# A hybrid decoder layer on one core: branch tiles read through a ring of five buffers, merge weights fetched earlier

## The chip, the cores and the metric

The kernel runs on one core of one Trainium2 chip. Its time is the device time of one execution in microseconds. Three runs of the kernel before took 1553.57, 1547.87 and 1562.55 us; the median, 1553.57 us, is the time to which everything is compared.

The names of the engines: PE is the matmul engine (PEld its weight load), ACT and DVE the two engines that copy, split and reduce, POOL a third such engine that also issues gathers, SP an engine that only issues transfers. ACT issues transfers too; "ACTq" and "SPq" in a row are an engine's issue of a transfer.

## The reference, cut to what matters

One inference step of one layer for a prompt of 512 tokens and, with the same weights, for 8 samples of one new token each that have 4096 past tokens in a paged cache. All is fp32.

```python
h = rmsnorm(x, g_norm1) * (1.0 + sc1) + sh1
u = einsum('btd,df->btf', h, w_in)
u_rx, u_ry, u_qkv, u_z, u_a, u_b, u_mq, u_mkv, u_gate = split(u, offs, axis=-1)
o_rg  = rglru_branch(u_rx, u_ry, ...)      # causal conv of width 4, gates, linear recurrence
o_gdn = gdn_branch(u_qkv, u_z, ...)        # causal conv of width 4, gated delta rule
cq   = rmsnorm(u_mq);  q = cq @ w_uq       # MLA_HEADS = 8, Q_LORA = 384
c_kv = rmsnorm(u_mkv[..., :256])           # keys c_kv @ w_uk, values c_kv @ w_uv
o_mla = attend(q_nope, q_rope, c_kv, k_rope, w_ukv)
m = (sigmoid(ga) * (o_rg @ w_rg_proj)      # 1280 -> 1024
     + sigmoid(gb) * (o_gdn @ w_gdn_proj)  # 1024 -> 1024
     + sigmoid(gc) * (o_mla @ w_mla_proj))
x = x + gt1 * (m @ w_o)                    # then the SwiGLU block
```

`attend` is causal attention over the 512 prompt tokens for the prompt, and for each sample attention over its 32 cache pages of 128 tokens and its own new token, in the latent space of 256 + 32 numbers.

## The kernel before, in words

Activations stand with features on the 128 partitions and the 520 tokens (512 of the prompt, 8 samples) along the free dimension, in two halves of 260. An fp32 product is made of three: each operand is split into a high and a low fp32r part, by a copy on ACT and a subtraction on DVE. `split` (L154) does so for a weight tile (`raw` to `whi` at L158 and `wlo` at L159), `hilo` (L175) for an activation tile (`brh` at L179, `brl` at L180). `load` (L149) fetches a weight tile into one of two buffers tagged `raw`; `wload` is load and split.

The program's parts in time, read from the trace:

- 0 to about 480 us: norm, the input projection and the gated delta branch. Every conv input tile takes its state of 35 columns by a copy at L383 (on POOL), 512 columns by ACT (L384) and 8 by DVE (L386).
- 480 to 735 us: the recurrent branch and the gate columns of the input projection. From here to about 985 us the sample attention runs in between, one step at a time: `steps(n)` adds n to what is due and runs as many steps of it. A step is, for instance, `scores` (L1107): 24 matmuls of a page block `cc` into the PSUM tile `sp`, a maximum (L1114, DVE) and a copy to SBUF (`SC`, L1115, ACT); or `sa`, the sum over pages `cv`. Pages come by SP (L1085) and, three of eight, as gathers by POOL (L1080); `cv` are gathers of POOL.
- 735 to 806 us: the MLA projections of the prompt. `bf` tiles of the latents (`d_ck`, `d_cq`) are read by SP through two buffers and split (ck0h, cq0h, ...); then `values` (L1293) with `w_uv`, then for four head pairs the keys with `w_uk` (L1335) and the queries with `w_uq` (L1342), each weight by a `wload` on ACT's queue.
- 806 to 914 us: prompt attention, a loop over 16 pairs of (head pair, query block) that runs two ahead with scores (`h` at L1359), one ahead with transposes (L1377), and then `ho` (L1387). In rounds 8 to 12 `branch` (L1277) reads a tile of the recurrent branch's output (`d_ro`) into one of two buffers `bf` and splits it.
- 914 to about 1040 us: the merges. `merge` multiplies the branch tiles by `w_rg` (ten k-tiles, two weight tiles of 640 columns for each of eight output tiles), then `w_gdn`, then `w_mla`, scaled by the gates (`tg`). `fetch` reads and splits the branch tiles just before each merge. After that come `w_o` and the SwiGLU block, to the end.

A tile scheduler fixes each engine's order of instructions at build time, and each engine runs its queue in that order. In the MLA and merge parts the weight and branch loads stand on ACT's queue, between ACT's copies; the page loads stand on SP's. Each load of SP or ACT signals one of eight semaphores, taken in turn, and where the load before on that semaphore might still be under way, the issuing engine first waits for it.

## Time and profile before

| what | value |
|---|---|
| median of 3 runs | 1553.57 us (1547.87 to 1562.55) |
| the profiled execution's own time | 1555.39 us |
| its span, first to last instruction | 1553.6 us |
| mean granted clock of PE | 0.975 of full speed |
| PE busy | 1479.3 us, 95% of the span |
| DVE, ACT, POOL busy | 818.9, 643.1, 243.2 us |
| mean transfer rate | 165 GB/s over the span |

The profiled execution is 1.82 us above the median of the three runs. A busy time is that of one engine; what an engine that is not the last to be ready spends idle costs nothing. The releaser in brackets is what ended the idle time in front of an instruction. The clock column gives the granted clock as a share of full speed.

### The profile page before, as it was taken

The page shows a single profiled execution, that of the slowest core. Times are in us where ns is not written, and L with a number is a line of the kernel's source. Part 1 is how long each engine was busy: PE and PEld are TensorE (multiplying, and loading weights), DVE is VectorE, ACT ScalarE, POOL GpSimd, SP SyncE. Part 2 cuts the span into 40 slices and gives each one's busy share as a digit, 9 for nine tenths or more (in the row PEclk, how much of TensorE's full clock was granted, in tenths as well). Part 3 has the DMA queues.
Part 4 walks back from the last instruction along what each step waited for, and adds up shares of the span by engine and source line. Part 5 has one row for each costly group of instructions (what it writes and reads, how often), then busy time and mean ns, then how long its engine had stood idle before and what let it go on. Part 6 is the DMA issues. An engine that isn't in the chain of part 4 may idle for free.

```text
span 1553.6 us, 33507 instructions
## 1 busy us (share of the span) xinstructions
PE 1479.3 (95%) x13348; PEld 1346.7 (87%) x13348; DVE 818.9 (53%) x1938; ACT 643.1 (41%) x1226; POOL 243.2 (16%) x391
## 2 busy tenths in 40 slices
PE   8999999999998999999878889999999999999997
PEld 5799999999987988887665559999999999999997
DVE  4577865857755676765344424464464333333333
ACT  4464644644533777564334433232243222222233
POOL 0121000100103444333323532000000000000001
PEclk7999999999998999999889999999999999999998
DMA  8234142351436966877777978676743223323222
GB/s 344 83 112 122 58 127 95 97 155 61 125 117 196 270 194 210 275 235 249 241 234 198 265 248 292 192 240 216 270 151 109 84 86 86 103 93 95 84 84 93
DMA packets 117774, 255.98 MB, mean 165 GB/s; under 512 B 22281, under 2 KB 53770, under 8 KB 117618
## 3 DMA queue, kind: packets, MB, share of 16 engines
q1 hardware_dynamic: 83904, 161.85, 33.0%
q0 software_dynamic: 13824, 47.72, 9.9%
q10 hardware_dynamic: 19890, 44.27, 8.8%
q8 instruction: 105, 1.72, 0.5%
q14 instruction: 51, 0.42, 0.1%
HBM read 228.61 MB, written 25.18 MB: 163 GB/s over the span
## 4 chain that ended last, share of the span: by engine, by line
PE 51%; DMA 4%; issue 2%; ACT 2%; DVE 1%; another core or an unknown queue 1%; SPq 0%; POOL 0%; ACTq 0%; POOLq 0%; DVEq 0%
PE mm L172 40%; PE sp L1112 2%; PE sa L1144 1%; DMA bf<-d_ro 1%; PE s L224 1%; PE ho L1387 1%; PE h L1359 1%; DMA St<-in_S 1%; PE mm L1312 1%; DMA bf<-d_cq 1%; PE h L1377 1%; DMA out_gS_s<-St 1%; PE s L888 1%; DMA raw<-in_w_rg 1%
## 5 line engine op out<-in xcount | busy, mean ns | idle before, releaser
L158 ACT ACTIVATE whi<-raw 128x1024 fp32r<-128x1024 f32 (+3 forms) x204 | 199.5, 979 | 506.9 <-PE mm L172 443.6
L159 DVE TENSOR_TENSOR wlo<-raw,whi 128x1024 fp32r<-128x1024 f32 (+3 forms) x204 | 229.1, 1124 | 232.4 <-ACT whi L158 226.4
L172 PE MATMUL mm<-hh,whi 128*128 128x260 f32 x1312 | 281.1, 292 | 4.9 <-ACT hh L295 2.7
L172 PE MATMUL mm<-hh,wlo 128*128 128x260 f32 x1312 | 273.5, 287 | 0.1
L172 PE MATMUL mm<-hl,whi 128*128 128x260 f32 x1312 | 272.9, 287 | 0.7 <-DVE hl L295 0.6
L172 PEld LDWEIGHTS mm<-hh,whi 128*128 128x128 f32 x1312 | 206.8, 191 | 16.6 <-issue 7.9
L172 PEld LDWEIGHTS mm<-hl,whi 128*128 128x128 f32 x1312 | 206.1, 191 | 3.2 <-issue 2.1
L172 PEld LDWEIGHTS mm<-hh,wlo 128*128 128x128 f32 x1312 | 206.1, 191 | 3.0 <-issue 1.4
L172 PE MATMUL mm<-h2h,whi 128*128 128x260 f32 x704 | 144.5, 284 | 0.0
L172 PE MATMUL mm<-h2h,wlo 128*128 128x260 f32 x704 | 144.1, 283 | 0.0
L172 PE MATMUL mm<-h2l,whi 128*128 128x260 f32 x704 | 143.6, 283 | 0.0
L1080 POOL DMA_INDIRECT cc<-in_ckvT,pkx x96 | 101.6, 1058 | 129.6 <-PE sp L1112 74.3
L172 PE MATMUL mm<-brh,whi 128*128 128x260 f32 x556 | 114.2, 287 | 5.1 <-ACT brh L179 4.9
L172 PE MATMUL mm<-brl,whi 128*128 128x260 f32 x556 | 113.0, 284 | 0.7 <-issue 0.6
L172 PE MATMUL mm<-brh,wlo 128*128 128x260 f32 x556 | 112.3, 284 | 0.0
L172 PEld LDWEIGHTS mm<-h2h,whi 128*128 128x128 f32 x704 | 109.3, 188 | 2.9 <-issue 2.5
L172 PEld LDWEIGHTS mm<-h2h,wlo 128*128 128x128 f32 x704 | 109.4, 188 | 0.4 <-issue 0.4
L172 PEld LDWEIGHTS mm<-h2l,whi 128*128 128x128 f32 x704 | 109.1, 188 | 0.4 <-DVE h2l L1549 0.4
L172 PEld LDWEIGHTS mm<-brh,whi 128*128 128x128 f32 x556 | 86.0, 189 | 11.0 <-ACT brh L179 6.0
L172 PEld LDWEIGHTS mm<-brl,whi 128*128 128x128 f32 x556 | 85.9, 189 | 1.6 <-DVE mx L1120 0.8
L172 PEld LDWEIGHTS mm<-brh,wlo 128*128 128x128 f32 x556 | 86.0, 189 | 0.3 <-issue 0.2
L1610 POOL TENSOR_TENSOR x<-x,rf 128x260 f32<-128x260 f32 x6 | 4.3, 736 | 514.7 <-ACT rf L1607 514.7
(522 smaller groups left out, 2500.7 us busy)
## 6 DMA issues: line engine op xcount, KB each, us to landing
raw<-in_w_in SPq DMA_DIRECT2D x55, 512.0 KB
wa<-in_w_ada SPq DMA_DIRECT2D x48, 512.0 KB
cc<-in_ckvT SPq DMA_DIRECT2D x160, 144.0 KB
raw<-in_w_f SPq DMA_DIRECT2D x44, 512.0 KB
raw<-in_w_in ACTq DMA_DIRECT2D x27, 512.0 KB
raw<-in_w_f SPq DMA_DIRECT2D x16, 384.0 KB
d_g<-gt ACTq DMA_DIRECT2D x22, 260.0 KB
raw<-in_w_rg ACTq DMA_DIRECT2D x16, 320.0 KB
```

What stands on the lines that cost most here:

```text
L158: A.activation(hi[:, :n], raw[:, :n], AF.Copy)
L159: V.tensor_tensor(lo[:, :n], raw[:, :n], hi[:, :n], ALU.subtract)
L172: TE.matmul(pt[:, a, 0:HB], w[:, k * 128:k * 128 + 128], x[k0 + k][:, a * HB:(a + 1) * HB], start=start and k == 0 and i == 0, stop=stop a ...
L224: TE.matmul(pt[32 * j:32 * j + 32, 0:256], sc[:, k, :], wa[:, j * 256:(j + 1) * 256], start=k == 0, stop=k == 7)
L888: TE.matmul(pw[:, 0:272], a_[:, sl], b_[:, ca], start=i == 0, stop=i == 2)
L1080: G.indirect_dma_start(ct[:, i].rearrange("p c t -> p (c t)"), None, I["ckvT"], bass.IndirectOffsetOnAxis(ap=pkx[0:96, o:o + 1], axis=0))
L1112: TE.matmul(po[32 * j:32 * j + 32, 0:256], Qst[:, t, 4 * self.g + j, :], cts[j][:, :, t, :], start=t == 0, stop=t == 2)
L1144: TE.matmul(self.pa[32 * j:32 * j + 32, 0:256], self.PTt[:, t * 128 + 32 * j:t * 128 + 32 * j + 32], self.vts[j][:, t * 256:(t + 1) * 256] ...
L1312: TE.matmul(pt[:, a, 0:256], a_[:, c0 + k * 128:c0 + k * 128 + 128], x[:, a * HB:a * HB + 256], start=k == 0 and i == 0, stop=k == n - 1 a ...
L1359: TE.matmul(pS[:, 0:n], qts[2 * p + u][:, b * 128:n], kts[p][:, u, 0:n], start=True, stop=False)
L1377: TE.transpose(pT[:, kb * 128:(kb + 1) * 128], Ps[u][:, kb * 128:(kb + 1) * 128], ident)
L1387: TE.matmul(po[u][:, b * 128:(b + 1) * 128], vv[:, kb, hd * 128:(hd + 1) * 128], PTs[u][:, kb * 128:(kb + 1) * 128], start=kb == 0, stop=k ...
```

## The change

What it does, in the order of the diff:

1. The copy of the conv state (L383) goes from POOL to DVE.
2. In a sample score step, ACT's copy of the PSUM tile comes first, and DVE takes the maximum from that copy in SBUF.
3. `branch` is cut in two: `branch_load` reads a tile into a ring, `branch` splits the oldest. During attention and the first merge the ring has five buffers in a pool of its own; ten `d_ro` and eight `d_og` loads are listed in `ahead`, and `send(1)` issues the next: in rounds 3 to 7 without a split, afterwards one for each split. The `d_og` tiles are split between the output tiles of the first merge, no longer in a block behind it. The 8 sample columns are copied by DVE, no longer by POOL.
4. The MLA weights have buffers of their own (four `ruk`, two `ruq`), filled ahead; the `w_uv` loads are named earlier; the latents' `bf` has three buffers. So the two `raw` buffers come free for the first two `w_rg` tiles.
5. In attention `steps(STEPS[1])` (0.7 of a step) also runs in the two rounds that fill the pipeline, so 1.4 steps more in all lie ahead of the loop's end.
6. `fetch` is used for the `d_om` tiles alone, with two buffers.

```diff
--- before.py
+++ after.py
@@ -380,7 +380,7 @@
 
             cin = p.tile([128, 548], F32, tag="cin", name="cin", bufs=2)
             y2 = p.tile([128, CW], F32, tag="cw", name="cz", bufs=6)
-            G.tensor_copy(cin[:, 0:35], state)
+            V.tensor_copy(cin[:, 0:35], state)
             A.activation(view2(cin[:, 35:547]), pt[:, :, 0:256], AF.Copy)
             seg = cin[:, 0:32].rearrange("p (a b c) -> p a b c", a=2, b=4)
             V.tensor_copy(seg[:, :, :, 3], pt[:, :, 256:260])
@@ -1111,8 +1111,8 @@
                     for j in range(4):
                         TE.matmul(po[32 * j:32 * j + 32, 0:256], Qst[:, t, 4 * self.g + j, :], cts[j][:, :, t, :],
                                   start=t == 0, stop=t == 2)
-                V.reduce_max(self.mx[:, blk:blk + 1], po[:, 0:256], axis=AX.X)
                 A.activation(self.SC[:, blk * 256:(blk + 1) * 256], po[:, 0:256], AF.Copy)
+                V.reduce_max(self.mx[:, blk:blk + 1], self.SC[:, blk * 256:(blk + 1) * 256], axis=AX.X)
 
             def weights(self):
                 st, mx, part = self.st, self.mx, self.part
@@ -1274,14 +1274,21 @@
     px = es.enter_context(pool("px"))
     xs = {}
 
-    def branch(p, n, src, k, samples):
-
-        f = p.tile([128, NT], F32, tag="bf", name="bf", bufs=2)
+    raw_ring = []
+
+    def branch_load(p, src, k, samples, bufs):
+
+        f = p.tile([128, NT], F32, tag="bf", name="bf", bufs=bufs)
         if samples is None:
             queue[0].dma_start(f, src[k])
         else:
             queue[0].dma_start(pr(f), src[k].rearrange("p (a b) -> p a b", a=2))
-            G.tensor_copy(sm(f), samples[:, k, :].rearrange("p (a b) -> p a b", a=2))
+            V.tensor_copy(sm(f), samples[:, k, :].rearrange("p (a b) -> p a b", a=2))
+        raw_ring.append(f)
+
+    def branch(p, n):
+
+        f = raw_ring.pop(0)
         xs[n] = hilo(px, f, "br", bufs=5) if n % 18 < 5 else hilo(p, f, "br", bufs=13)
 
     with ExitStack() as sub:
@@ -1291,7 +1298,7 @@
         kts, qts = [], []
 
         def values(lat):
-            uvs = [wload(I["w_uv"][c], 1024) for c in range(2)]
+            uvs = [split(r, 1024) for r in raws]
             for b in range(4):
                 pt = mm_tile()
                 for c in range(2):
@@ -1319,9 +1326,24 @@
             csq = pl.tile([128, 2, 512], F32, name="csq")
             krp = pl.tile([128, 512], F32, name="krp")
             lat = {}
+
+            raws = [load(I["w_uv"][c], 1024) for c in range(2)]
+            ruk, ruq = [], []
+
+            def key_load(p):
+                ruk.append(pl.tile([128, 256], F32, tag="ruk", name="ruk", bufs=4))
+                queue[0].dma_start(ruk[-1], I["w_uk"][p])
+
+            def query_load(p):
+                ruq.append(pl.tile([128, 768], F32, tag="ruq", name="ruq", bufs=2))
+                queue[0].dma_start(ruq[-1], I["w_uq"][p])
+
+            for p in range(2):
+                key_load(p)
+                query_load(p)
             for nm, src, n in (("ck", d_ck, 2), ("cq", d_cq, 3)):
                 for i in range(n):
-                    f = pl.tile([128, NT], F32, tag="bf", name="bf", bufs=2)
+                    f = pl.tile([128, NT], F32, tag="bf", name="bf", bufs=3)
                     SP.dma_start(f, src[i])
                     lat[nm, i] = hilo(pl, f, f"{nm}{i}", bufs=1)
             SP.dma_start(csq, I["csq"])
@@ -1332,14 +1354,17 @@
             V.tensor_copy(mbf[:, 1], pt[:, 0:128])
             values(lat)
             for p in range(4):
-                pt = lat_gemm(lat, wload(I["w_uk"][p], 256), 0, "ck", 2)
+                pt = lat_gemm(lat, split(ruk[p], 256), 0, "ck", 2)
                 kt = ph.tile([128, 2, 512], F32, name=f"kt{p}")
                 for u in range(2):
                     lo_, hi_ = slice(64 * u, 64 * u + 64), slice(64 - 64 * u, 128 - 64 * u)
                     A.activation(view2(kt[lo_, u]), pt[lo_, :, 0:256], AF.Copy)
                     V.tensor_copy(kt[hi_, u], krp[hi_])
                 kts.append(kt)
-                wq = wload(I["w_uq"][p], 768)
+                wq = split(ruq[p], 768)
+                if p < 2:
+                    key_load(p + 2)
+                    query_load(p + 2)
                 for u in range(2):
                     pt = lat_gemm(lat, wq, u * 384, "cq", 3)
                     qt = ph.tile([128, 512], F32, name=f"qt{p}{u}")
@@ -1348,6 +1373,15 @@
                 steps(STEPS[5])
 
         pp = sub.enter_context(pool("pp"))
+
+        pr_ = smp.enter_context(pool("pr", side="right"))
+        ahead = [(d_ro, k, None) for k in range(10)] + [(d_og, k, osf) for k in range(8)]
+
+        def send(n):
+            for a in ahead[:n]:
+                branch_load(pr_, *a, 5)
+            del ahead[:n]
+
         psum(sub, "psh", h=4, ho=2)
         spare[0] = lambda: s_tile("h")
 
@@ -1400,11 +1434,14 @@
                 PTs[i + 1] = turn(order[i + 1][1], Ps.pop(i + 1))
             if i + 2 < 16:
                 Ps[i + 2] = scores(*order[i + 2])
+            steps(STEPS[1])
             if i < 0:
                 continue
-            steps(STEPS[1])
+            if 3 <= i < 8:
+                send(1)
             if 8 <= i < 13:
-                branch(pp, i - 8, d_ro, i - 8, None)
+                branch(pp, i - 8)
+                send(1)
             if b == 3:
                 for u in range(2):
                     om = pp.tile([128, 512], F32, tag="om", name="om", bufs=2)
@@ -1418,9 +1455,10 @@
     with ExitStack() as sub:
         pg = sub.enter_context(pool("pg"))
 
-        def fetch(n, src, k0, k1, samples):
-            for k in range(k0, k1):
-                branch(pg, n + k, src, k, samples)
+        def fetch(n, src, samples):
+            for k in range(8):
+                branch_load(pg, src, k, samples, 2)
+                branch(pg, n + k)
 
         def merge(n, nk, w, gate0, first, then=None):
 
@@ -1442,9 +1480,15 @@
                 if then is not None:
                     then(d)
 
-        fetch(0, d_ro, 5, 10, None)
-        merge(0, 10, "w_rg", 0, True)
-        fetch(10, d_og, 0, 8, osf)
+        for n in range(5, 10):
+            branch(pg, n)
+            send(1)
+
+        def next_tile(d):
+            branch(pg, 10 + d)
+            send(1)
+
+        merge(0, 10, "w_rg", 0, True, next_tile)
         merge(10, 8, "w_gdn", 8, False)
         steps(99)
         smp.close()
@@ -1468,7 +1512,7 @@
             mhl.append(hilo(wm, macc[d], "ma", bufs=8))
             ada(1 + d % 2)
 
-        fetch(18, d_om, 0, 8, omS)
+        fetch(18, d_om, omS)
         merge(18, 8, "w_mla", 16, False, then)
```

How the instructions stand now. First ACT in the MLA projections; `kt` are the keys, `whi<-raw` of 256 columns the split of a `w_uk` tile, of 768 a `w_uq` tile. Before:

```order
L1339 ACTIVATE kt_10725<-mm 64x512 x2
L158 ACTIVATE whi<-raw 128x256
L151 DMA raw<-in_w_uq 128x768
L1115 ACTIVATE SC<-sp 128x256
L151 DMA raw<-in_w_uk 128x256
L158 ACTIVATE whi<-raw 128x768
L151 DMA raw<-in_w_uq 128x768
L1137 ACTIVATE PT<-s 128x512
L1115 ACTIVATE SC<-sp 128x256
L158 ACTIVATE whi<-raw 128x256
```

Now, in the stretch ahead of the latents' splits (ck0h, ck1h, cq0h), which were the start of that part before too:

```order
L375 DMA d_g<-gt 128x520
L1114 ACTIVATE SC<-sp 128x256
L151 DMA raw<-in_w_rg 128x640
L1121 ACTIVATE SC,st<-SC,mx 128x1024
L1151 ACTIVATE opt<-sa 128x256
L1335 DMA ruk<-in_w_uk 128x256
L1339 DMA ruq<-in_w_uq 128x768
L1335 DMA ruk<-in_w_uk 128x256
L1339 DMA ruq<-in_w_uq 128x768
L179 ACTIVATE ck0h<-bf 128x520
L179 ACTIVATE ck1h<-bf 128x520
L179 ACTIVATE cq0h<-bf 128x520
```

Before, each weight tile was loaded a few rows ahead of its split, when one of the two `raw` buffers was free. Now two `w_rg` tiles, two `ruk` and two `ruq` are issued ahead of the first split of a latent.

Next ACT at the start of the prompt attention; `brh<-bf` is a split of a branch tile, `Pt` the softmax, `PTm` the copy of a transpose. Before, from the second split on:

```order
L151 DMA raw<-in_w_rg 128x640
L1365 ACTIVATE Pt,mxp<-h,mxp 128x256
L1281 DMA bf<-d_ro 128x520
L1365 ACTIVATE Pt,mxp<-h,mxp 128x256
L1379 ACTIVATE PTm<-h 128x256
L1115 ACTIVATE SC<-sp 128x256
L1281 DMA bf<-d_ro 128x520
L1379 ACTIVATE PTm<-h 128x256
L179 ACTIVATE brh<-bf 128x520 x2
L1365 ACTIVATE Pt,mxp<-h,mxp 128x384
L1281 DMA bf<-d_ro 128x520
L1365 ACTIVATE Pt,mxp<-h,mxp 128x384
```

Now, from the last two splits of the head weights to the first two of a branch tile:

```order
L151 DMA raw<-in_w_rg 128x640
L158 ACTIVATE whi<-raw 128x640
L1283 DMA bf<-d_ro 128x520 x3
L1399 ACTIVATE Pt,mxp<-h,mxp 128x128 x2
L1232 ACTIVATE of<-sa 128x256
L1283 DMA bf<-d_ro 128x520
L1413 ACTIVATE PTm<-h 128x128 x2
L1283 DMA bf<-d_ro 128x520
L1399 ACTIVATE Pt,mxp<-h,mxp 128x256 x2
L1137 ACTIVATE PT<-h 128x512
L179 ACTIVATE brh<-bf 128x520
L1114 ACTIVATE SC<-sp 128x256
```

Before, a branch load followed a split, two at a time. Now five loads of branch tiles stand ahead of the first split, and the next loads follow two splits each.

Last PE at the start of the MLA projections; `sp<-cc,Qst` and `s<-cst,SC` belong to the sample attention, `mm<-whi,ck0h` is the first product of `values`. Before:

```order
L1144 MATMUL sa<-cv,PT 32x256 x16
L1331 MATMUL s<-cst 128x128
L1112 MATMUL sp<-cc,Qst 32x256 x9
L1135 MATMUL s<-cst,SC 128x128 x4
L1112 MATMUL sp<-cc,Qst 32x256 x3
L1135 MATMUL s<-cst,SC 128x128 x3
L1112 MATMUL sp<-cc,Qst 32x256 x6
L1301 MATMUL mm<-whi,ck0h 128x512 x2
L1301 MATMUL mm<-wlo,ck0h 128x512 x2
```

Now:

```order
L1144 MATMUL sa<-cv,PT 32x256 x16
L1353 MATMUL s<-cst 128x128
L1112 MATMUL sp<-cc,Qst 32x256 x9
L1135 MATMUL s<-cst,SC 128x128 x4
L1112 MATMUL sp<-cc,Qst 32x256 x3
L1308 MATMUL mm<-whi,ck0h 128x512 x2
L1308 MATMUL mm<-wlo,ck0h 128x512 x2
L1308 MATMUL mm<-whi,ck0l 128x512 x2
L1308 MATMUL mm<-whi,ck1h 128x512 x2
```

Three transposes `s<-cst,SC` and six matmuls `sp` that stood ahead of `values` now come behind its start.

## Rows read from the trace of the kernel before

**Rows 1.** The page: busy us of each engine (share), instructions.

```profile
PE 1479.3 (95%) x13348; PEld 1346.7 (87%) x13348; DVE 818.9 (53%) x1938; ACT 643.1 (41%) x1226; POOL 243.2 (16%) x391
```

**Rows 2.** Stretches: length, busy time of each engine (instructions), PE clock, DMA share, GB/s.

```profile
740.00:940.00 200.00, 166.46 (x1397) 116.74 (x1392) 80.26 (x224) 75.81 (x179) 75.40 (x80) 0.91 0.79 241
940.00:1540.00 600.00, 599.91 (x5124) 581.93 (x5123) 254.59 (x418) 176.05 (x245) 11.90 (x21) 1.00 0.44 141
```

**Rows 3.** Waits of ACT, 740 to 940: total us, times, longest.

```profile
ACT brh L179 <- DMA bf<-d_ro: 17.2, 5, 6.0
...
ACT SC L1115 <- DVE mx L1114: 7.4, 5, 2.8
```

**Rows 4.** Timeline of ACT and its queue: start, duration, instruction, [idle before, releaser].

```profile
735.35 0.36 ACTq L375 DMA_DIRECT2D d_g<-gt  x1
738.73 0.33 ACTq L151 DMA_DIRECT2D raw<-in_w_uq  x1
...
767.97 0.34 ACTq L151 DMA_DIRECT2D raw<-in_w_uk  x1
...
782.92 0.42 ACT L158 ACTIVATE whi<-raw 128x256 fp32r<-128x256 f32 x1 [4.94 <-remote]
```

**Rows 5.** Timeline of PE, 784 to 794 us.

```profile
784.47 0.80 PE L1312 MATMUL mm<-cq0h,whi 128*128 128x256 f32 x2 [6.12 <-ACT kt L1339]
785.07 0.63 PE L1312 MATMUL mm<-cq0l,whi 128*128 128x256 f32 x2
...
788.61 2.09 PE L1112 MATMUL sp<-cc,Qst 96*32 96x256 f32 x24
...
792.71 0.40 PE L1312 MATMUL mm<-ck0l,whi 128*128 128x256 f32 x2
```

**Rows 6.** Timeline of ACT, the split of the first merge weights.

```profile
806.09 1.56 ACT L158 ACTIVATE whi<-raw 128x640 fp32r<-128x640 f32 x2 [2.85 <-DMA raw<-in_w_rg]
```

**Rows 7.** Timeline of PE, 808 to 831 us.

```profile
808.74 0.49 PE L1359 MATMUL h<-kt,qt 128*128 128x128 f32 x2 [2.18 <-DVE qt L1346]
...
820.09 1.50 PE L1112 MATMUL sp<-cc,Qst 96*32 96x256 f32 x24
826.18 0.87 PE L1377 MATMUL h<-cst,Pt 128*128 128x128 f32 x3 [4.59 <-DVE mxp L1363]
...
828.86 1.92 PE L1359 MATMUL h<-kt,qt 128*128 128x512 f32 x2
...
830.67 1.16 PE L1359 MATMUL h<-kt,qt 128*128 128x512 f32 x2
```

**Rows 8.** Timeline of ACT, 918 to 925 us.

```profile
918.36 0.82 ACTq L1281 DMA_DIRECT2D bf<-d_ro  x2
...
924.70 1.29 ACT L179 ACTIVATE brh<-bf 128x520 fp32r<-128x520 f32 x2 [5.96 <-DMA bf<-d_ro]
```

**Rows 9.** Timeline of PE, 925 to 930 us.

```profile
925.39 0.80 PE L172 MATMUL mm<-brh,whi 128*128 128x260 f32 x2 [4.43 <-ACT brh L179]
926.12 1.92 PE L1144 MATMUL sa<-cv,PT 128*32 128x256 f32 x10
...
930.18 1.49 PE L1144 MATMUL sa<-cv,PT 128*32 128x256 f32 x20
```

**Rows 10.** Timeline of SP's queue, 717 to 741 us.

```profile
717.48 22.08 SPq L1085 DMA_DIRECT2D cc<-in_ckvT  x14
739.68 0.84 SPq L1325 DMA_DIRECT2D bf<-d_ck  x2
```

**Rows 11.** Timeline of PE, the start of the MLA part.

```profile
739.55 1.48 PE L1112 MATMUL sp<-cc,Qst 96*32 96x256 f32 x18 [2.16 <-ACT SC L1115]
...
746.98 1.99 PE L1112 MATMUL sp<-cc,Qst 96*32 96x256 f32 x12 [2.24 <-issue]
```

**Rows 12.** Lines 383 and 386: count, ns min/median/max, first and last start.

```profile
L383 POOL COPY cin<-gst x24: 211/213/1050, 66.4 to 394.2; 128x35 f32<-128x35 f32 x24
...
L386 DVE COPY cin<-mm x34: 152/165/174, 73.5 to 668.2; 128x8 f32<-128x8 f32 x34
```

## The prediction

> **What bounds the kernel now.** I read the busy times first: PE works 1479.3 of 1553.6 us [rows 1], so what any change of waits can win is at most the rest, some 74 us. Then the stretches: from 940 to 1540 us PE is busy for 599.91 of 600 us at full clock, while from 740 to 940 us it is busy for 166.46 of 200 us at a clock of 0.91 [rows 2]. The 33.5 idle us of that one stretch are nearly half of all that PE idles, and it is where the change moves loads; the transfer engines there have a share of 0.79 at 241 GB/s [rows 2]. Then the waits and the timelines, in order of time. In each the reader should see what PE waited for, follow that back to a transfer, and then look at the matmuls behind the wait: they run slower than the same matmuls later.
>
> - 778 to 789 us. ACT's load of a `w_uk` tile is issued at 767.97, and its split starts only at 782.92, after 4.94 us idle [rows 4]. PE waits 6.12 us for the keys made from it. Behind the wait a pair of 256-column matmuls takes 0.63 where the same pair takes 0.40 later, and 24 matmuls of `sp` take 2.09 [rows 5] against 1.50 [rows 7]: nine pairs by about 0.19 (their starts are 0.42 apart, later 0.24) and 0.6, so 2.3 us of low clock.
> - 806 to 811 us. ACT splits the first two `w_rg` tiles after 2.85 us of waiting for them [rows 6]; DVE stands behind it, and PE waits 2.18 us for a `qt` [rows 7].
> - 821 to 831 us. Branch tiles: between 740 and 940 us five waits of ACT for `d_ro` sum to 17.2 us [rows 3], three of them here. The softmax is held behind one, and PE waits 4.59 us; then two score matmuls of 512 columns take 1.92 where the next two take 1.16 [rows 7]. With the others I put the low clock at 1.5 us.
> - 917 to 930 us. A pair of branch tiles is issued at 918.36, when the two buffers come free, and split at 924.70 [rows 8]. PE waits 4.43 us, and ten `sa` matmuls take 1.92, where twenty take 1.49 four us later [rows 9]: some 1.2 us of low clock there and 0.8 in the matmuls around, 2 in all.
>
> **The change, part by part.** The sum is made against the profiled execution's own 1555.4 us, which is 1.8 us above the median of three.
>
> *Own buffers for `w_uk`, `w_uq`* (gain 0 to 8.4, taken 6.5). The first two pairs are issued before the first latent is split, the last two `w_uk` tiles right behind the third latent's, and none waits for a `raw` buffer any more. The 6.12 and the 2.3 us go, less what is late next: the third `w_uq` tile has only two buffers and is issued after the first one's split, and `sa` at 790 needs gathers that were issued after 772. I take off 2.
>
> *Head weights ahead* (0 to 3, taken 2.5): they are in SBUF long before 806, so the 2.18 us and a smaller wait behind go.
>
> *Ring of five in attention* (0 to 6.7, taken 6): 4.59 us, 0.6 of smaller waits and 1.5 of clock. Against it: the first split now stands two softmax rounds behind five loads of 266 KB, so the first may be late; but the two loads issued at the same place before were split without such a wait, and the next are asked for later.
>
> *Ring in the merge* (0 to 7.5, taken 7): at the merge's start five tiles lie ready, so the block at 918 to 925 goes: 4.43 us, 1.1 of smaller waits, 2 of clock.
>
> *Latents with three buffers* (0 to 1.4, taken 1): three waits of about half a microsecond in `values`.
>
> *Maximum from the copy* (-1 to 2.2, taken 1). Before, ACT's copy waited for DVE's maximum 5 times, 7.4 us in all [rows 3], and PE once waited 2.16 us for the copy [rows 11]. Now the bank is free after the copy alone; the maximum comes later, but only four blocks later is it needed.
>
> *More steps in the fill* (0 to 0.5, taken 0): they fill gaps that close anyway.
>
> Gains: 6.5 + 2.5 + 6 + 7 + 1 + 1 = 24 us.
>
> *Conv state by DVE* (-1 to 7 us lost, taken 0.5). 34 copies leave POOL, where one took 0.21 us. The nearest DVE row is 0.165 us for eight columns [rows 12]; with 35 I take 0.18, or 6 us of DVE in all, on an engine that is busy for 53% [rows 1]. What hides it is that PE has other gemms in flight; if that cover were gone, all 6 to 7 us would show. The 16 copies of sample columns that also leave POOL are 2.6 us of DVE by the same row, spread over the merges, and I cost them at nothing there: the merges' gemms on PE cover them.
>
> *The start of the MLA part* (0 to 4 lost, taken 2). It is not relieved: SP issues the two `d_ck` loads at 739.68, behind 22 us of page loads [rows 10], and the splits of these tiles come only after. Ahead of them ACT now issues two `w_rg` tiles and two pairs of `ruk`, `ruq`, 1.66 MB by their shapes where there were 0.5. The transfer engines at their full share carry 241/0.79 = 305 GB/s, so 1.15 MB more is 3.8 us if all of it goes first, and nothing if none does. Also the last `sp` block, 1.99 us at 746.98 after 2.24 idle [rows 11], has moved behind `values`: PE waits that much longer and does it later.
>
> Here a rule can be weighed. The Trainium skill, "DMA: Bandwidth & Descriptors", section "Queues, rings and completion order", says that each transfer engine takes turns between the queues that have work, a packet at a time; its section "Issuing engines are not separate DMA queues" adds that all issuers end on the same 16 engines. By that, ACT's extra bytes take their turn against the latents' and the pages' and delay them even though they are on another queue: the loss would be nearer 4 than 2, and the forecast 2 us higher. The w_uk tile above agrees: 128 KB were 15 us under way beside pages and gathers.
>
> *ACT's issues* (0 to 41 lost, taken 1.5). Each load waits for its semaphore. At 735.35 and 738.73 stand two issues of ACT [rows 4], 3.4 us apart, with the copies behind held meanwhile. Twelve loads of the branch and head kind now stand between ACT's copies from 806 to about 840 us, against nine; if none is held they cost nothing, if all are, 41 us. I take half of one, since in the attention before no issue of this kind shows such a hold.
>
> *Transfers fuller* (0 to 5, taken 1): below.
>
> Losses: 0.5 + 2 + 1.5 + 1 = 5. Net 19, and 1555.4 - 19 = **1536 us**.
>
> **The rivals.**
>
> *The waits come back as transfer waits (R1).* No byte is saved, 24 us of time is. The stretch moves 241 GB/s for 200 us, 48 MB; in 176 us that is 274 GB/s, a share of 0.90. On the mean that is still below what the engines carry, which speaks against a hard bound; for it speaks that page gathers of POOL and page loads of SP run in the same stretch, and that small waits for pages already stand between the large ones. If half of the gain is turned into waits for `cc`, `cv` or late branch tiles: 1555.4 - 12 + 5 = 1548.
>
> *All of it is won (R2).* The losses stay at nothing and the low clock goes altogether: 8.4 + 3 + 6.7 + 7.5 + 1.4 + 1 = 28, so 1527.
>
> *ACT is held by its issues (R3), slower.* From 806 to 840 us, softmax, transposes' copies and `SC` copies of ACT stand behind a row of loads, and PE lives on them. A load of the ring needs a free buffer (a DVE subtraction) and its semaphore (the load eight before, in a stretch where loads take up to 15 us). At 3.4 us a time the point from which it decides is 24/3.4, seven of the twelve loads held on the path; all twelve give 1555.4 + 41 - 24 = 1572. For it speaks the row at 738.73, against it that ACT is busy for 76 of 200 us there [rows 2] and that the same kinds of loads before were not held.
>
> *The change does not do what it says at one place*: the scheduler has put the ring's first split close behind its loads, and the stall of 821 comes at 812 instead. That costs the 6 us of the ring in attention, 1542, within the forecast's range.
>
> **How the numbers follow.** Forecast 0.46 (1529 to 1545), R1 0.32 (1545 to 1556), R2 0.11 (1524 to 1529), R3 0.11 (1556 to 1575). About 1%, 15.5 us, is what a measurement of this kernel can tell from no change; from the median that is below 1538 or above 1569. The sum's 1536 counts from a run 1.8 above the median, so the forecast lies just beyond that line: about 0.33 of its 0.46 falls below, with R2 0.44; of R3 0.07 is above 1569. Faster 0.45, same 0.48, slower 0.07. The range leaves out the upper R3 and a little of R1 above, and the lower end of R2: 1525 to 1554. The forecast alone: 1529 to 1545.
>
> **What would show it.** Right: no PE wait of over 2 us for `kt`, `qt`, `brh` or a softmax between 775 and 935 us of the old time; the granted clock of that stretch at 0.97 or more; PE idle there at 12 to 15 us. The start: the first `values` matmul at least as late as 748.9, and idle time before it of over 5 us. R1: new idle rows at `sp` or `sa`, released by `cc` or `cv`, and a transfer share above 0.9. R3: ACT rows after a load with an idle time of over 2 us "issue". DVE copies: idle of ACT or PE behind L386 in the first 480 us above today's. The prediction is wrong if the stretch is shortened and the time is not, or if the first 735 us change by more than 5 us.

## The result: slower by three quarters of a per cent, and the profile after

The changed kernel took 1566.13 us (median of 20 runs, 1556.5 to 1573.83), the kernel before beside it 1555.94 us (20 runs). The ratio is 1.0075, with a 95% interval of 1.0056 to 1.0093. The forecast was 1536 us with a range up to 1554, so it had the wrong sign and the result lies outside the range. By the line of about 1% that the prediction drew, this still counts as "same", though the interval does not contain 1. The profiled execution of the changed kernel took 1563.83 us, its span is 1562.0 us; the two profiled executions differ by 8.4 us, the medians by 10.2.

The page's first row, in the columns of [rows 1]:

```profile
PE 1478.9 (95%) x13348; PEld 1346.2 (86%) x13348; DVE 822.8 (53%) x1988; ACT 643.3 (41%) x1226; POOL 218.8 (14%) x341
```

PE does the same work in the same busy time; what grew is its idle time. The two stretches of [rows 2], now:

```profile
740.00:940.00 200.00, 163.65 (x1396) 113.95 (x1393) 79.38 (x232) 74.77 (x179) 78.25 (x81) 0.92 0.81 250
940.00:1540.00 600.00, 597.11 (x5083) 579.43 (x5084) 252.89 (x416) 174.43 (x240) 4.27 (x4) 1.00 0.43 139
```

The stretch on which the forecast of 19 us rested has kept its idle time and its low clock: 163.65 us busy where it was 166.46, and a clock of 0.92 where it was 0.91.

Where the time went is read by cutting each trace at the same instructions of PE. "Recurrent" runs from the first to the last matmul `s<-xch` of L888. "MLA" runs from the end of the last gate matmul to the end of the last projection. "Attention and first merge" goes on from there to the first matmul of the `w_gdn` merge.

| us, one profiled execution each | before | after | difference |
|---|---|---|---|
| up to the recurrent part | 503.1 | 502.2 | -0.9 |
| recurrent | 198.1 | 203.9 | +5.8 |
| rest of the gates | 32.8 | 32.3 | -0.5 |
| MLA | 72.3 | 83.6 | **+11.3** |
| attention and first merge | 185.7 | 179.9 | -5.9 |
| from there to the last matmul | 554.3 | 553.0 | -1.3 |

The working of the prediction, sorted by the same cuts, would have been +0.5, then -6.5 in MLA and -13 in attention and first merge. So less than half of the gain behind the projections came, and the MLA part, where a gain was forecast, lost 11.3 us.

The 11.3 us can be cut further. From the last gate matmul to the first matmul of `values` it is 14.9 us before and 15.6 after, so little is lost ahead of `values`. From there to the first matmul of a key it is 14.3 and 21.7 us, and from that to the last projection 43.1 and 46.4. Of the 7.4 us in `values`, 4.8 are more idle time of PE.

ACT and its queue in the MLA part of the changed kernel (columns as in [rows 4]):

```profile
743.12 0.34 ACTq L151 DMA_DIRECT2D raw<-in_w_rg  x1
...
745.78 0.33 ACTq L1335 DMA_DIRECT2D ruk<-in_w_uk  x1
...
750.94 0.33 ACTq L1339 DMA_DIRECT2D ruq<-in_w_uq  x1
753.18 0.64 ACT L179 ACTIVATE ck0h<-bf 128x520 fp32r<-128x520 f32 x1 [7.02 <-DMA bf<-d_ck]
756.26 0.64 ACT L179 ACTIVATE ck1h<-bf 128x520 fp32r<-128x520 f32 x1 [2.44 <-DMA bf<-d_ck]
...
758.95 0.36 ACTq L1335 DMA_DIRECT2D ruk<-in_w_uk  x1
...
768.37 0.64 ACT L179 ACTIVATE cq1h<-bf 128x520 fp32r<-128x520 f32 x1 [5.72 <-DMA bf<-d_cq]
769.07 0.64 ACT L179 ACTIVATE cq2h<-bf 128x520 fp32r<-128x520 f32 x1
769.61 1.92 ACT L1310 ACTIVATE vv<-mm 128x1024 f32<-128x1024 f32 x2
```

The same splits of latents in the kernel before:

```profile
746.82 0.63 ACT L179 ACTIVATE ck0h<-bf 128x520 fp32r<-128x520 f32 x1
...
755.54 0.64 ACT L179 ACTIVATE cq0h<-bf 128x520 fp32r<-128x520 f32 x1 [0.98 <-DMA bf<-d_cq]
757.98 0.64 ACT L179 ACTIVATE cq1h<-bf 128x520 fp32r<-128x520 f32 x1 [1.80 <-DMA bf<-d_cq]
```

SP's queue, which carries the latents, now:

```profile
722.47 22.11 SPq L1085 DMA_DIRECT2D cc<-in_ckvT  x14
744.62 1.31 SPq L1347 DMA_DIRECT2D bf<-d_ck  x2
...
756.32 2.99 SPq L1347 DMA_DIRECT2D bf<-d_cq  x2
```

And before, where the first `d_ck` load went at 739.68 [rows 10]:

```profile
748.21 0.93 SPq L1325 DMA_DIRECT2D bf<-d_cq  x2
```

PE, first before and then now:

```profile
748.90 1.22 PE L1301 MATMUL mm<-whi,ck0h 128*128 128x512 f32 x2
```

```profile
753.87 1.22 PE L1308 MATMUL mm<-whi,ck0h 128*128 128x512 f32 x2 [4.14 <-issue]
...
770.67 1.22 PE L1308 MATMUL mm<-whi,ck0h 128*128 128x512 f32 x2 [4.93 <-ACT vv L1310]
...
799.99 0.79 PE L1319 MATMUL mm<-cq0h,whi 128*128 128x256 f32 x2 [6.92 <-ACT kt L1361]
```

Read them together. The `d_ck` loads are issued at 744.62, behind 22 us of page loads as before, and the weight loads of ACT go out on both sides of them. ACT then stands 7.02 us for the first latent. Later it stands 5.72 us for `cq1`, whose split was at 757.98 in the trace of before and is at 768.37 here; counted from the end of the gate matmuls (734.0 and 738.3) that is 6.1 us later. Its load is both issued later, at 756.32, and longer under way: by the updates of the load's semaphore in the trace 12.0 us, where it was 9.1 before. In ACT's queue the copies `vv<-mm` stand behind that split, though they have nothing to do with it: PE has filled its PSUM buffers and waits 4.93 us for a copy that waits for a load. Behind that wait PE is also slow: the pair of 512-column matmuls that takes 1.22 us at 770.67 takes 0.63 at 775.08, and from 770 to 775 us the granted clock is 0.50, its lower level (1.2 GHz). The last row is the old wait at 784 [rows 5] come back; it is taken up below.

The transfer share of the same program, by stretches:

```profile
738.00:768.00 30.00, 19.56 (x124) 11.38 (x122) 6.79 (x15) 7.26 (x12) 9.64 (x10) 0.83 1.03 317
771.00:783.00 12.00, 12.00 (x74) 9.71 (x77) 2.58 (x5) 4.51 (x8) 0.00 (x0) 0.83 0.11 34
```

The share is the next to last column. The engines are full for 30 us, and just after they are nearly empty for 12. Before, they were full too (1.03 from 740 to 755 us), but the empty stretch behind was short (0.06 from 760 to 765). POOL's next gather of a page says why:

```profile
783.76 1.56 POOL L1080 DMA_INDIRECT cc<-in_ckvT,pkx  x1 [29.99 <-PE sp L1112]
```

It waits 30 us for a page buffer (the same wait was 16.73 us before), which comes free when PE runs `sp` matmuls, and the twelve of [rows 11] at 746.98 now stand behind the start of `values`. SP issues no page load from 767.7 to 783.5 us either. So what the crowd cost is not won back by an emptier stretch: the page loads could not use it.

### The profile page after: what moved, and what is told of

Same layout as the page of the kernel before. It is cut to its first block, busy times and chain, and to the rows that moved or that the text cites. A ratio compares the mean times of both kernels' runs of the same rounds, so it can differ in the third digit from the quotient of the medians.

```text
span 1562.0 us, 33439 instructions
## 1 busy us (share of the span) xinstructions
PE 1478.9 (95%) x13348; PEld 1346.2 (86%) x13348; DVE 822.8 (53%) x1988; ACT 643.3 (41%) x1226; POOL 218.8 (14%) x341
## 4 chain that ended last, share of the span: by engine, by line
PE 75%; DVE 7%; ACT 6%; DMA 6%; issue 3%; another core or an unknown queue 1%; SPq 0%; POOL 0%; ACTq 0%; POOLq 0%; DVEq 0%
PE mm L172 57%; PE sp L1112 3%; PE sa L1144 2%; PE mm L1319 1%; PE s L224 1%; ACT whi L158 1%; PE ho L1421 1%; DMA raw<-in_w_in 1%; DVE wlo L159 1%; PE s L888 1%; DMA ruk<-in_w_uk 1%; PE h L1393 1%; PE h L1411 1%; DMA cc<-in_ckvT 1%
## 5 line engine op out<-in xcount | busy, mean ns | idle before, releaser
L158 ACT ACTIVATE whi<-raw 128x1024 fp32r<-128x1024 f32 (+2 forms) x196 | 194.8, 995 | 519.5 <-PE mm L172 461.5
L159 DVE TENSOR_TENSOR wlo<-raw,whi 128x1024 fp32r<-128x1024 f32 (+2 forms) x196 | 223.6, 1142 | 220.4 <-ACT whi L158 213.7
```

The source lines that it names most:

```text
L158: A.activation(hi[:, :n], raw[:, :n], AF.Copy)
L159: V.tensor_tensor(lo[:, :n], raw[:, :n], hi[:, :n], ALU.subtract)
```

## Experiments

The runs were made on four chips, on one of which the kernel before takes 1540 us instead of 1554 to 1556. Each ratio is therefore against runs of the kernel before on the same chip, and parts are compared on the same chip where it matters. An expected time in us is compared as a ratio where the chip was another. "Part" figures are from one profiled execution each; two profiles of one kernel on two chips (before and b0, after and a0) agree within 2.3 us in the recurrent part and 0.8 us in the two others, and within 2.0 us in `values`. The stretch ahead of the recurrent part, which only edit 1 touches, is 499.1 to 509.1 us long in these profiles, so one profile's total says little. "Values" is the stretch from the first matmul of `values` to the first of a key, a piece of the MLA part.

| kernel | ratio, 95% interval | recurrent | MLA | of it values | attention, first merge |
|---|---|---|---|---|---|
| after | 1.0075 (1.0056 to 1.0093) | 203.9 | 83.6 | 21.7 | 179.9 |
| u12 | 1.0040 (1.0013 to 1.0067) | 197.4 | 82.7 | 18.8 | 177.8 |
| u4 | 1.0063 (1.0036 to 1.0091) | 202.7 | 79.0 | 20.9 | 183.8 |
| ring | 1.0019 (0.9987 to 1.0050) | 195.8 | 76.3 | 19.3 | 186.1 |
| b12 | 0.9998 (0.9970 to 1.0025) | 204.4 | 69.1 | 14.7 | 183.2 |
| b0 (before again) | | 195.8 | 72.7 | 16.3 | 186.0 |
| a0 (after again) | 1.0087 (1.0058 to 1.0117) | 202.5 | 82.8 | 22.7 | 180.7 |
| hold | 1.0004 (0.9980 to 1.0029) | 203.1 | 70.6 | 13.2 | 185.1 |
| hold12 | 0.9982 (0.9955 to 1.0010) | 197.4 | 67.3 | 14.7 | 181.8 |
| u1 | 1.0089 (1.0059 to 1.0119) | 206.2 | 83.7 | 19.4 | 179.1 |
| u2 | 1.0059 (1.0036 to 1.0082) | 198.8 | 83.3 | 21.6 | 183.3 |
| u5 | 1.0083 (1.0052 to 1.0113) | 201.2 | 84.3 | 22.8 | 183.0 |
| late2 | 0.9964 (0.9939 to 0.9988) | 196.8 | 73.5 | 13.7 | 178.8 |
| *the fast chip:* b1 | 0.9996 (0.9974 to 1.0019) | 190.2 | 75.2 | 15.2 | 180.1 |
| dummy | 1.0093 (1.0061 to 1.0124) | 188.2 | 87.3 | 24.2 | 176.1 |
| ringlate | 0.9975 (0.9951 to 0.9999) | 188.0 | 75.0 | 17.7 | 178.3 |
| late | 0.9932 (0.9907 to 0.9957) | 188.8 | 75.4 | 17.1 | 168.4 |

### Undoing parts, and doing parts alone

**u12**: the changed kernel with edits 1 and 2 undone.

```diff
-            V.tensor_copy(cin[:, 0:35], state)
+            G.tensor_copy(cin[:, 0:35], state)
...
+                V.reduce_max(self.mx[:, blk:blk + 1], po[:, 0:256], axis=AX.X)
                 A.activation(self.SC[:, blk * 256:(blk + 1) * 256], po[:, 0:256], AF.Copy)
-                V.reduce_max(self.mx[:, blk:blk + 1], self.SC[:, blk * 256:(blk + 1) * 256], axis=AX.X)
```

> The changed kernel with the state copy back on POOL and the maximum back on the PSUM tile. Theory L (these two edits made the recurrent part 5.8 us longer, 502 to 706 us where it was 503 to 701): the recurrent part ends near 701 again and the time is 1560, 6 us below the changed kernel's 1566. Rival (the order of that part moved for other reasons, or the part varies by that much from run to run): the time stays at 1566 and the part ends at 706.

It is still slower than before, by 0.40%. That is 0.35% less than the changed kernel, but the two intervals overlap, so the gain in time is not shown. The recurrent part falls to 197.4 us, as the theory had it; the MLA part stays at 82.7.

**u4**: the changed kernel with edit 4 undone (`wload` for `w_uk` and `w_uq`, no early `w_uv`, two `bf`).

```diff
-            uvs = [split(r, 1024) for r in raws]
+            uvs = [wload(I["w_uv"][c], 1024) for c in range(2)]
...
-                wq = split(ruq[p], 768)
+                wq = wload(I["w_uq"][p], 768)
```

> The changed kernel without the MLA part of the edit: w_uk, w_uq and w_uv load through the two raw buffers again, the latents through two, and so the w_rg head tiles are not ahead. Theory M (1.15 MB more ahead of the latents made `values` 8 us and the projections 3 us longer): values take 14 us instead of 21.8, the projections 43, and the time is 1555. Rival (the latents are late because the part before is late, or because the last sample block moved behind values): values still take over 20 us and the time stays at 1564 to 1566.

It is no clean undoing. With the places in ACT's queue free, the scheduler moved the ring's `d_ro` loads up to 744 to 758 us, ahead of the latents, where the weight loads had been, and the MLA part is at 79.0 us. `values` takes 20.9 us, as the rival had it, but with other loads in the same place this does not decide between the two.

**ring**: the kernel before with the ring alone (edits 3 and 6).

> The kernel before with the ring of five raw buffers for the branch tiles alone (and its d_og tiles split between the output tiles of the first merge). Theory R (the ring is what won 7 us between the end of attention and the end of the w_rg merge, and it costs nothing elsewhere): 1548. Rival (the ring wins in the merge only what its loads take in attention): 1554 to 1557.

ACT's queue in it:

```profile
748.55 0.33 ACTq L1283 DMA_DIRECT2D bf<-d_ro  x1
...
749.22 0.33 ACTq L1283 DMA_DIRECT2D bf<-d_ro  x1
...
751.26 1.42 ACTq L1283 DMA_DIRECT2D bf<-d_ro  x2
...
760.44 0.64 ACT L179 ACTIVATE cq0h<-bf 128x520 fp32r<-128x520 f32 x1 [3.88 <-DMA bf<-d_cq]
763.96 0.64 ACT L179 ACTIVATE cq1h<-bf 128x520 fp32r<-128x520 f32 x1 [2.88 <-DMA bf<-d_cq]
```

Loads that the program writes in attention have gone out some 60 us ahead of it: the new pool had free buffers then. The latents of the queries are late, `values` takes 19.3 us, and no gain is left: 1.0019, as the rival had it.

**b12**: the kernel before with edits 1 and 2.

> The kernel before with the state copy on DVE and the maximum taken from the SBUF copy, nothing else. Theory L: the recurrent part is 5 to 6 us longer and the time is 1561. Rival (these two cost nothing, what was lost there is the order): 1556 or a little less.

No difference in the whole, as the rival had it, though the recurrent part is 6 to 9 us longer, as the theory had it. The MLA part with the attention is 6 us shorter: the wait of 6.12 us for `kt` [rows 5] is not in this trace (the longest at that place is 0.63 us). Nothing shows that the edits removed it.

**b1**: the kernel before with edit 1 alone.

> The kernel before with the state copy on DVE alone. In the three kernels with state copy and maximum both changed the recurrent part took 203 to 204 us with 12 to 14 us idle, in the three without 196 to 198 with 8. Theory L1 (it is the copy, in DVE's queue ahead of the other work): 203 us or more. Rival L2 (it is the maximum, which now waits in DVE's queue for ACT's copy): 198 us as before. The time: 1555 to 1560 by L1, 1555 by L2.

No difference. Edit 1 by itself costs nothing that can be told, and its price was right: in the changed kernel a copy at L383 takes DVE a median of 0.183 us, where the estimate was 0.18.

### The crowd at the start of the MLA part

**dummy**: the kernel before, with five loads of 266 KB that nobody reads, on ACT's queue ahead of the latents' splits.

```diff
+            for k in range(5):
+                x = pl.tile([128, NT], F32, tag="xtra", name="xtra", bufs=5)
+                queue[0].dma_start(x, d_ro[k])
```

> The kernel before with five more loads of 266 KB (branch tiles that nothing reads) issued by ACT just ahead of the split of the first latent; all else as it was. Theory M2 (whatever is loaded ahead at that place, head weights, MLA weights or branch tiles, delays the latents d_cq, for which ACT and behind it PE wait): values take 19 to 20 us instead of 14.3 and the time is 1560. Rival (the bytes are harmless; values got longer in the other kernels by the order of the sample blocks): values 14 to 15, time 1555.

The MLA part goes to 87.3 us from 75.2 in b1 on the same chip, and the whole time up by 0.93%, 14 us, for 1.33 MB; `values` takes 24.2 us, more than the theory's 19 to 20. ACT:

```profile
740.26 4.56 ACTq L1324 DMA_DIRECT2D xtra<-d_ro  x4
744.87 0.64 ACT L179 ACTIVATE ck0h<-bf 128x520 fp32r<-128x520 f32 x1 [7.43 <-DMA bf<-d_ck]
...
759.43 0.64 ACT L179 ACTIVATE cq0h<-bf 128x520 fp32r<-128x520 f32 x1 [10.92 <-DMA bf<-d_cq]
760.56 0.64 ACT L179 ACTIVATE cq1h<-bf 128x520 fp32r<-128x520 f32 x1 [0.49 <-DMA bf<-d_cq]
761.10 1.92 ACT L1303 ACTIVATE vv<-mm 128x1024 f32<-128x1024 f32 x2
```

PE:

```profile
745.56 1.22 PE L1301 MATMUL mm<-whi,ck0h 128*128 128x512 f32 x2 [6.79 <-ACT ck0h L179]
...
762.16 1.22 PE L1301 MATMUL mm<-whi,ck0h 128*128 128x512 f32 x2 [9.06 <-ACT vv L1303]
```

SP's queue:

```profile
746.33 3.75 SPq L1085 DMA_DIRECT2D cc<-in_ckvT  x3
750.63 2.38 SPq L1328 DMA_DIRECT2D bf<-d_cq  x2
```

The same two waits as in the changed kernel: for the first latent, and for `vv` copies that stand behind a late split. Only the second makes the loss. In b1, without the loads, ACT waits 5.34 us for the first latent too, and the first matmul of `values` comes 17.5 us behind the gates here and 18.0 there.

Nor is this the loss by bytes alone. In b1 two `d_cq` loads go out at 745.04, ahead of the page loads, and the first `vv` copy stands ahead of the splits of `cq0` and `cq1`. With the loads added, the scheduler put three page loads ahead of the `d_cq` loads and both splits ahead of that copy. By their semaphores the first four latent loads are under way no longer than in b1: 8.5, 9.8, 8.8 and 7.9 us against 9.2, 10.7, 8.5 and 7.6. What made the `d_cq` tiles late in dummy is their later issue, 22.6 us behind the gates where b1 has 18.7. How the loss divides between the loads and the new order is not shown.

**ringlate**: `ring`, with the ring's loads held by an order edge behind ACT's last copy of a key.

```diff
+                    anchor = A.activation(view2(kt[lo_, u]), pt[lo_, :, 0:256], AF.Copy)
...
+                with tc.issue_after(anchor.ins):
+                    branch_load(pr_, *a, 5)
```

> The ring of five alone, as in the run before, but its loads may be issued only after ACT's last copy of a key tile, so none of them stands ahead of the latents. Theory M2: values are back at 14 to 15 us, the rest stays as with the ring, and the time is 1550 to 1551. Rival: values stay at 19 us, or what they win is lost again at the start of attention, where the loads now stand in a row: 1556.

With the loads held back the ring gains 0.25%, at the edge of what is told from nothing. `values` takes 17.7 us, not the 14 to 15 that were expected; b1 on this chip has 15.2.

**late**: `ringlate` with edit 5 (the sample steps in the two fill rounds).

```diff
+            steps(STEPS[1])
             if i < 0:
                 continue
-            steps(STEPS[1])
```

> The ring with its loads held back behind the last key copy, and the sample steps in the pipeline's fill; state copy on POOL, maximum from PSUM and the MLA loads as before. Theory: recurrent part 198 us, values 14, attention 107 to 108 with the extra sample steps, w_rg merge 72 instead of 78: 1547 to 1549, the best of all so far. Rival (the merge's gain is only sample work that moved into attention): 1553 to 1556.

0.9932, a little better than expected: it beats both kernels. Its gain over `ringlate` lies in attention and first merge, 168.4 against 178.3 us, though the two intervals overlap.

**b0** and **a0** are the kernels before and after once more, on the chip of the two that follow.

> The kernel before once more, for a profile from the same chip as the three kernels beside it. Its parts should be as in the first profile: recurrent 188 to 198 us, values 14 to 15, projections 42 to 43, attention 104 to 108, w_rg merge 76 to 78.

> The changed kernel once more, beside the kernel before on the same chip: 1.0075 of it, values 6 to 8 us longer, w_rg merge 6 us shorter, recurrent part 2 to 6 us longer.

Both came as expected, within about 2 us of each band.

**hold**: the changed kernel, in which only the first `ruk`, `ruq` pair goes ahead of the latents. The other MLA weights and the `w_rg` tiles stand behind the last latent's split, the ring's loads behind the last key copy.

```diff
+            hold[:] = split_of
+            with tc.issue_after(hold[0].ins):
+                key_load(1)
+                query_load(1)
```

> The changed kernel with the same buffers and edits, but of the loads ahead only the first w_uk, w_uq pair may be issued before the splits of the latents; the other MLA weights and the two w_rg tiles come behind the last latent's split, the ring's loads behind the last key copy. Theory M2: values 14 to 17 us instead of 21, and 0.5 to 0.8% less than the changed kernel, 1.000 of the kernel before or a little under. Rival (the changed kernel loses by the deferred sample blocks and the edits 1 and 2, not by its loads): within 0.2% of the changed kernel.

The MLA part falls from 82.8 us (a0) to 70.6, `values` from 22.7 to 13.2, and the time from 1.0087 to 1.0004; the two intervals are apart. Of the rest of the MLA part's fall, 4.14 us is a0's wait for `kt`, which is not in this trace. ACT:

```profile
745.13 0.34 ACTq L1338 DMA_DIRECT2D ruk<-in_w_uk  x1
...
751.73 0.63 ACT L182 ACTIVATE ck1h<-bf 128x520 fp32r<-128x520 f32 x1
752.90 0.64 ACT L182 ACTIVATE cq0h<-bf 128x520 fp32r<-128x520 f32 x1 [0.55 <-DMA bf<-d_cq]
761.36 1.03 ACT L1313 ACTIVATE vv<-mm 128x1024 f32<-128x1024 f32 x1 [7.82 <-PE mm L1311]
762.28 0.63 ACT L182 ACTIVATE cq1h<-bf 128x520 fp32r<-128x520 f32 x1
```

Now ACT waits for PE, and not PE for ACT: no split of a latent waits longer than 0.55 us here. By their semaphores the loads of `cq1` and `cq2` are under way 7.5 and 9.8 us, where it is 13.2 and 11.2 in a0, and `cq1`'s is issued 13.8 us behind the gates, where it is 16.7. What was late next is a gather, at 754.45, where PE waits 6.81 us for `cv`. Of the gain behind the projections 4 to 5 us are lost with the later loads (185.1 against 180.7 us).

The rival of the expectation, that sample matmuls moved behind `values` cause the loss, can be read from the traces. Before, 56 `sp` matmuls stand between the gates and `values`, in the changed kernel 44. hold has 46 and not the loss; ring and u4 have 62, and `values` takes 19.3 and 20.9 us there. So the moved matmuls are neither enough for the loss nor needed for it. The edit of hold touches the loads alone, but the scheduler also moved one page load from ahead of two `d_cq` loads to behind them, and two sample copies of ACT ahead of the latents' splits, so crowding and order are not told apart here either.

**hold12**: `hold` with edits 1 and 2 undone.

> The same with the state copy back on POOL and the maximum from PSUM. Theory L (those two cost 0.35% in the changed kernel, all of it in the recurrent part): 0.35% below the kernel without this undoing, 0.993 to 0.997 of the kernel before. Rival (they cost only where the start of the MLA part is already late): the same time as without it.

0.9982: against `hold` the recurrent part is shorter by 5.7 us, the time by 0.2%, with overlapping intervals and short of the band that the theory gave.

### The recurrent part, and the merge

**u1**: the changed kernel with edit 1 undone. **u2**: with edit 2 undone.

> The changed kernel with the copy of the conv state back on POOL; the maximum still comes from the copy in SBUF. With both edits undone the ratio to the kernel before was 1.0040, with neither 1.0075. Theory (the maximum in DVE's queue waits for ACT's copy and holds what stands behind it): 1.006 to 1.008, recurrent part still 201 to 205 us. Rival (34 copies more on DVE are the cost): 1.004 to 1.005, recurrent part 196 to 199 us.

> The changed kernel with the maximum taken from PSUM again, ahead of ACT's copy; the conv state is still copied by DVE. Theory (the maximum): 1.003 to 1.005, recurrent part 196 to 199 us. Rival (the DVE copies): 1.006 to 1.008, recurrent part 201 to 205 us. If both kernels come out near 1.0055 the two share it; if both keep 1.0075 only the pair of them does it.

The recurrent part is 206.2 us with the maximum from the copy and 198.8 us with the maximum from PSUM, whichever engine copies the state. On the three slower chips the seven profiles with edit 2 have 201 to 206 us and the seven without 195 to 199. So the 6 us are the maximum's. The times stand in the order that the theory gave, each above its band (1.0089 and 1.0059), but their intervals overlap, and u2's is nearer to the rival's band, 1.006 to 1.008. One place where it seems to act is this. DVE in the changed kernel:

```profile
623.50 0.60 DVE L1016 SCALAR_TENSOR_TENSOR kul<-kuh,cst,s 128x128 fp32r<-128x128 f32 x2
624.02 0.41 DVE L1115 TENSOR_REDUCE mx<-SC 128x1 f32<-128x256 f32 x1
624.35 0.68 DVE L1019 TENSOR_TENSOR um<-kul,cst 128x512 fp32r<-128x512 f32 x1
```

PE, and then the same instruction of PE in u1:

```profile
625.18 0.49 PE L1025 MATMUL s<-um,kul 24*128 24x512 f32 x2 [1.97 <-DVE um L1019]
```

```profile
626.57 0.49 PE L1025 MATMUL s<-um,kul 24*128 24x512 f32 x2 [3.75 <-DVE um L1019]
```

Before, the maximum came as soon as `sp` was done (at 617.45 in that trace, ahead of the same DVE work). Now it comes after ACT's copy and stands between `kul` and `um`. The same wait of PE is 0.78 us in the trace of before and 0.19 us in u2. But it does not follow the edit: it is absent in a0, u4, b12, hold and u5, which have edit 2, and u12, which has not, waits 2.75 us at such a place (687.5). So it does not account for the 6 us. What most of the seven share is a longer wait of PE's `s<-xch` matmuls for ACT's tanh (`t`, L889): 4.5 to 5.8 us in after, u4, b12, hold and u5, against 0 to 3.1 in the seven without; in a0 and u1 it is 1.0 or less. How the maximum brings the 6 us about stays open.

**u5**: the changed kernel with edit 5 undone.

> The changed kernel with steps(STEPS[1]) back behind the test of i < 0, so that the two rounds that fill the attention pipeline run no sample steps. Theory (the gain of 6 us in the first merge comes from the sample work that these calls move out of it): first merge 79 to 84 us instead of 72, attention 3 to 5 us shorter, ratio 1.009 to 1.012. Rival (the ring brings it, as predicted): first merge stays at 71 to 73 us, ratio 1.005 to 1.0075.

The boundary moved as the theory had it: the first merge's matmuls take 85.0 us from their first one on, and 71.8 in the changed kernel; attention is 9 us shorter for it (94.7 against 103.5 us), more than the 3 to 5 expected. But the time, 1.0083, cannot be told from that of the changed kernel, so neither theory's band is excluded. What the ring leaves in the merge without these steps shows on ACT:

```profile
927.98 4.52 ACTq L1285 DMA_DIRECT2D bf<-d_og  x3
932.54 0.64 ACT L179 ACTIVATE brh<-bf 128x520 fp32r<-128x520 f32 x1 [4.28 <-DMA bf<-d_om]
...
946.07 0.99 ACTq L151 DMA_DIRECT2D raw<-in_w_rg  x2
...
953.85 1.52 ACT L158 ACTIVATE whi<-raw 128x640 fp32r<-128x640 f32 x2 [6.10 <-DMA tg<-d_g]
```

and on PE:

```profile
931.31 0.51 PE L172 MATMUL mm<-brl,whi 128*128 128x260 f32 x2 [2.32 <-DVE brl L180]
...
954.64 0.80 PE L172 MATMUL mm<-brh,whi 128*128 128x260 f32 x2 [3.68 <-ACT whi L158]
```

The wait for branch tiles [rows 9] has shrunk to 2.32 us, and the longest wait is now one for the merge's own weights. The row at 953.85 names a gate tile, `tg`, whose load was issued just behind; by its semaphore the weight tile issued at 946.07 landed at 953.77, right before the split. These loads stand on the same queue behind `d_og` loads that the ring sends early. That the `d_og` loads delay them is read from the order of the queue; no run isolates it.

**late2**: `late` once more, on another chip.

> The same kernel as late: the kernel before with the ring of five and the step calls in the fill rounds, the ring's loads held behind ACT's last key copy; edits 1, 2 and 4 undone. Theory (its gain is in the merge and does not hang on the chip): 0.991 to 0.996. Rival (it hung on a chip on which the kernel before took 1540 instead of 1554): 0.997 to 1.002.

0.9964, a shade outside the band of 0.991 to 0.996 that the theory gave, and faster than before by its whole interval. On both chips `late` beats both kernels.

## Why the prediction was wrong, by its own steps

**The step that failed: "The start of the MLA part (0 to 4 lost, taken 2)".** The mechanism stood there, that ACT's new loads go out beside the latents; its size did not. It was priced as the transfer time of the bytes added, 3.8 us at most. (By their shapes the six tiles are 1.70 MB, not 1.66; that moves the bound by 0.1 us.) The MLA part lost 11.3 us, 7.4 of them in `values`. The price of a late tile is not its transfer: behind its split on ACT stand the `vv` copies, behind them PE, and behind PE the pages, for which the transfer engines then stood at 0.11. hold, whose edit changes only where the early loads may be issued, takes the loss away in `values` and in the whole time: that the early loads are the cause is shown. How much of it is crowding on the transfer engines and how much the order that the scheduler chose with them is not. By the Trainium skill, "DMA: Bandwidth & Descriptors", section "Queues, rings and completion order", the queues that have work take turns on a transfer engine, from which I had concluded that another queue's bytes delay the latents. a0 against hold agrees in sign (the load of `cq1` is 13.2 us under way against 7.5), dummy against b1 does not show it, and the loss goes past the 4 us that I had put beside that sentence.

**"Own buffers for w_uk, w_uq" (0 to 8.4, taken 6.5)** failed too, by its premise. It read the wait of 6.12 us for `kt` [rows 5] as a wait for a load issued 15 us earlier [rows 4], and took the 15 us for the load's time under way. The last update that the trace has of the load's semaphore is at 774.1, 6 us after the issue and 9 us before the split. In the changed kernel the same tile, the third `w_uk`, is loaded at 758.95 and its split comes at 798.44, 40 us later; PE waits 6.92 us all the same. ACT around it:

```profile
794.12 0.38 ACT L1114 ACTIVATE SC<-sp 128x256 f32<-128x256 f32 x1 [7.23 <-PE mm L1319]
798.44 0.42 ACT L158 ACTIVATE whi<-ruk 128x256 fp32r<-128x256 f32 x1 [3.93 <-remote]
```

In both kernels the split's releaser is given as "remote". That should have been read as "the profile does not know" and not as the load next to it. The semaphores in the trace say a little more: the split waits for two, the load's and PE's, and the last to change is PE's, at 782.89 and 798.41, 4.5 and 5.3 us behind the end that the trace gives for PE's last matmul before it. Why it comes so late stays open. The wait is 3.9 to 7.2 us long in eleven of the eighteen profiles and under 0.7 in the others: hold, hold12, b12 and the four on the fast chip. So b12 is without it, with no buffers of its own, and has an MLA part of 69.1 us beside 70.6 in hold and 67.3 in hold12. What the buffers are worth is not shown.

**"Maximum from the copy" (-1 to 2.2, taken 1)** left out a part of the program. It looked only at the waits between 740 and 940 us, where the bank was late. In the recurrent part the edit costs 6 us, which is beyond its lower end of -1; that the work behind the maximum on DVE waits with it is argued, not shown. In the whole time a loss is not shown: edits 1 and 2 together make 0.35% in the changed kernel and 0.2% in hold, both with overlapping intervals, and b12, without the rest of the change, loses nothing.

**"Ring in attention" (taken 6), "ring in the merge" (7), "head weights" (2.5)**: 15.5 us were forecast before the losses of 2.5 by issues and fuller transfers; 5.9 came. In attention the term holds where edit 5 is absent: from the last projection to the last `ho` it is 104.6 us before, 94.7 in u5 and 100.2 in ring. In the merge it does not: from the last `ho` to the `w_gdn` merge it is 81.2 us before and 88.3 in u5, 86.0 in ring, with the same number of sample matmuls in it. In u5 the rows above show part of the reason, a new wait for `w_rg` in the place of the old one for branch tiles; in ring no single wait of over 1.8 us was found. With edit 5, in the changed kernel, that stretch is 76.4 us. What the head weights by themselves won was not measured.

**"More steps in the fill" (0 to 0.5, taken 0)** may have been mis-sized where the loads are held back. From ringlate to late it is 0.39% of the time (1534.44 to 1528.51 us, but the intervals overlap) and 10 us of the two parts; in the changed kernel it takes 13 us out of the merge, puts 9 into attention, and wins nothing that can be measured.

**"Conv state by DVE" (0.5)** and **the rest of the program (0)** were right as far as can be told: b1 is 0.9996, with an interval that a loss of 0.5 us cannot be read from, and the last 550 us are 1.3 us shorter.

**The rivals.** R3, the slower one, was built on ACT's issues holding ACT's copies. One such hold is in the trace, two loads of `d_ro` at 836.78 that take 3.52 us, with the softmax behind them. That is far from the seven that it needed. The sign was R3's, but the mechanism was not: copies were held, by splits that waited for late loads, and at the other end of the stretch. So the chance of 0.11 that stood on R3 was met by luck. "The change does not do what it says at one place" came true in ring and u4, where the scheduler drew the ring's loads ahead of the latents.

Some of the signs that were named tell it: the granted clock of 740 to 940 us stayed at 0.92 where 0.97 was asked for, PE's idle time there is 36.35 us where 12 to 15 were, and the wait for `kt` is still over 2 us. The sign of the start does not: the first `values` matmul came at 753.87, as late as asked for, but 4.3 us of that had been lost before the gates ended, and after 4.14 us of idle time where over 5 were asked for.
